# The recurrence's keys loaded once, operand splits spread among other work, and folded weights copied and stored in another way

## The chip, the core and the metric

The kernel runs on one core of a Trainium2 chip. The metric is the device time of one execution in microseconds (us). TensorE (PE in the profile) multiplies, VectorE (DVE), ScalarE (ACT) and GpSimd (POOL) work on tiles, and SP's queue issues most DMAs; ScalarE and GpSimd have DMA queues of their own, which issue a few. Each engine runs its instructions in the order in which they stand in its queue, and an instruction that waits holds what stands behind it.

## The reference, cut to what matters

One layer: a joint input projection, whose columns feed a sliding-window attention with sinks and a gated linear recurrence, an output projection, a cross-attention to 256 memory tokens, and a SwiGLU feed-forward. `T = 2048` tokens, `D = 1024`, float32.

```python
u = rms_norm(h, g_mix_pre);  z = u @ w_in
qa, ka, va, qh, fh, ih, gh = jnp.split(z, IN_SPLITS, axis=-1)
y = concat(swa_with_sinks(qa, ka, va, sinks), hgrn2(qh, fh, ih, gh, ...)) @ w_out
h = h + rms_norm(y, g_mix_post)
u = rms_norm(h, g_x_pre);  m = rms_norm(mem, g_mem)
h = h + rms_norm(cross_attention(u, m, wq_x, wk_x, wv_x, wo_x), g_x_post)
u = rms_norm(h, g_ffn_pre)
h = h + rms_norm((silu(u @ w_gate) * (u @ w_up)) @ w_down, g_ffn_post)
```

In the recurrence, per head and chunk of 64 tokens, with `b` the running sum of the log decays in the chunk:

```python
A = jnp.where(causal, einsum((qc * exp(b - b_mid)), (kc * exp(b_mid - b))), 0.0)
kv = einsum(kc * exp(b_last - b), vc)          # S = decay * S + kv
o = A @ vc + (qc * exp(b)) @ S_prev
```

## The kernel before, in words

Tokens are worked on in pairs of chunks, 128 tokens, `n = 0..15` (8 per half, "block" of 1024 tokens). Every float32 product is made of three products of float32r operands: an operand is split into an upper part, a rounded copy (`hi`), and a lower part, the difference (`lo`). The copy is an ACTIVATE on ScalarE or an operation on GpSimd, the difference is always on VectorE. A product of upper by upper, upper by lower and lower by upper goes into one PSUM bank (`mm3`, lines 170 to 172 for projections; `products`, lines 1107 to 1109 in the later stages).

The program has these stages, by time: the input projection of block 0 (`in_first`); the input projection of block 1 (`in_proj`) with the sliding-window attention (`swa`) and the recurrence (`hgrn`) of block 0 between its columns; the attention of block 1 beside the rest of `in_proj`; the recurrence of block 1 beside `fold_cross`; and then `phases`, a long run of products with the output projection, the folded cross-attention and the feed-forward, in a form with seven products where eight would be usual.

`fold_cross` multiplies weights by the normalised memory so that the cross-attention needs only two products per token: it normalises and transposes the memory into `mT` (lines 131 to 134), projects it with `wk_x` in 8 columns of 24 products of 256 columns each (line 150 splits the weight on ScalarE, line 153 on VectorE, lines 303 and 304 split the result `kv`), multiplies by `wq_x` into `qk_d` (line 326 copies the result into an `x` tile, line 328 stores it from ScalarE's queue), projects with `wv_x`, and multiplies by `wo_x` into `vo_d`: per head two rows of two banks, which line 364 copies into an `x` tile on ScalarE and line 365 stores from ScalarE's queue. Differences of parts of `qk` are stored in `qk_s` too.

`hgrn` takes one pair through several steps. In `hgrn_front`, `k1` and `kk` are two copies of the same keys, loaded from `z_d`; `k1` (one buffer) goes into the products with the queries (line 867), whose banks `copy_predicated` (line 868, VectorE) and a copy (line 869, ScalarE) empty into `atz`; `kk` is scaled in place on GpSimd (line 876) and transposed (line 879) into `kt` (line 881), the values `v` are transposed (line 884) into `vt` (line 886). `hgrn_state` multiplies `kt` by `vt` (line 896), `hgrn_out` and `hgrn_last` make the output.

`swa_back` copies its result into the tile `ys` (lines 833 and 834), which is stored to `y_d`; `ys` has one buffer. `w_sums` (line 1018) makes sums and differences of parts of `w_out`, in `x` tiles, and stores them in `w_s`.

`phases` begins with a prologue: eight steps that load halves of four operands of the output projection (`w_out` and `w_s`) into `z` tiles and split them into resident tiles `T` (lines 971 and 974). `mix` calls them after the recurrence. Then come the streamed operands, loaded from `y_d` into `sraw` tiles and split into `S`, which the first products of the stage need.

A scheduler sets the order of each queue: it takes instructions as their operands come ready in its own timeline and by the order in which they were traced, so that an instruction that is traced late can stand early. `mark()` notes the last instruction traced so far on ScalarE, VectorE, TensorE and SP, and what is traced inside `behind()` stays behind that instruction on each of these. A tile with `bufs=n` has n buffers, and a new tile waits until what used its buffer n tiles earlier is done. A PSUM bank is freed by the instruction that empties it. `io_tile("x")` has three buffers, `io_tile("z")` two.

Of the kernel before, what the change touches and what calls it, by code (L numbers as in the profile page):

```python
# [11 lines left out]
F32 = mybir.dt.float32  # L12
F32R = mybir.dt.float32r
I32 = mybir.dt.int32
AF = mybir.ActivationFunctionType
ALU = mybir.AluOpType
AX = mybir.AxisListType

P = 128
T = 2048  # L20
D = 1024
# [8 lines left out]
NT = T // P  # L30
# [3 lines left out]
C_KA, C_VA, C_QH, C_FH, C_IH, C_GH = 512, 640, 768, 1280, 1792, 2304  # L34
# [14 lines left out]
class Layer:  # L49
# [155 lines left out]
    def mix(self):  # L205
        tc, I = self.tc, self.I
        kw = dict(reuse_waits="tile")
        with contextlib.ExitStack() as left:
            def pool(name, at, **k):
                return at.enter_context(tc.tile_pool(name=name, bufs=1, **k, **kw))  # L210

            self.mc = pool("mc", left)
            self.r_x = self.cst.tile([P, NT], F32, name="r_x")
            with (
                tc.tile_pool(name="t1", bufs=3, **kw) as self.ts,
                tc.tile_pool(name="t2", bufs=3, **kw) as self.tb,
                tc.tile_pool(name="s1", bufs=2, side="right", **kw) as self.st_pool,
                contextlib.ExitStack() as at,
            ):
                self.banks(at, "ps1", **MOST)  # L220
                self.raws, self.parts, self.sums = 3, 3, 3
                u = self.in_first()
            self.banks(left, "ps2", **FOUR)
            self.hg = pool("hg", left)
            self.wp = pool("wp", left)
            self.io = pool("io", left)
            with tc.tile_pool(name="sw", bufs=1, side="right", **kw) as self.sw:
                self.zero_tiles()
                swa = self.swa(range(NPB), "st")
                hgrn = self.hgrn(range(NPB), "h")  # L230
                cols = self.in_proj(1, u)
                for _ in range(2):
                    next(cols)
                for _ in swa:
                    for _ in range(5):
                        next(hgrn)
                    next(cols)
                for _ in hgrn:
                    pass
                jobs = self.jobs()  # L240
                sums = self.w_sums()
                swa = self.swa(range(NPB, NT), "sth")
                for i, _ in enumerate(swa):
                    next(cols)
                    if i:
                        self.mark()
                        for _ in range(4):
                            next(sums, None)
                for _ in cols:
                    pass  # L250
                for _ in sums:
                    pass
            phases = self.phases(jobs, None, lambda: self.io_tile("z"))
            with tc.tile_pool(name="xp", bufs=1, side="right", **kw) as self.xp:
                fold = self.fold_cross()
                for i, _ in enumerate(self.hgrn(range(NPB, NT), "gt")):
                    for _ in range(1 if i % 5 else 0):
                        next(fold)
                for _ in range(8):
                    next(phases)  # L260
                for _ in fold:
                    pass
            left.close()
            with (
                tc.tile_pool(name="t3", bufs=3, **kw) as self.ts,
                tc.tile_pool(name="t4", bufs=3, **kw) as self.tb,
                tc.tile_pool(name="s3", bufs=2, side="right", **kw) as self.st_pool,
                contextlib.ExitStack() as at,
            ):
                self.banks(at, "ps3", **MOST)  # L270
                self.raws, self.parts, self.sums = 6, 4, 5
                for _ in phases:
                    pass
# [9 lines left out]
    def fold_cross(self):  # L283

        nc, ph = self.nc, self.xp
# [30 lines left out]
        for d in (0, 4, 1, 5, 2, 6, 3, 7):  # L316
            th, tl = self.wcols(self.I["wq_x"], d, "A")
            o = self.io_tile("x")
            for q in range(2):
                ps = self.bank("sh"[q])  # L320
                for r in range(2):
                    h = 2 * q + r
                    self.mm3(ps[:, r * M:(r + 1) * M],
                             [((th[:, j, :], tl[:, j, :]), (kT[0][:, j, :], kT[1][:, j, :])) for j in (2 * h, 2 * h + 1)])
                sl = slice(q * 512, (q + 1) * 512)
                nc.scalar.activation(o[:, sl], ps, AF.Copy, scale=gx[:, d:d + 1])
                if q:
                    self.put(self.qk_d[d * P:(d + 1) * P, :], o)
                yield
            if d < 4:  # L330
                upper = o
                continue
            a, b = [ph.tile([P, D], F32, tag="qs", name=f"qs{d}_{i}", bufs=2) for i in range(2)]
            l, r = slice(0, 512), slice(512, D)
            nc.vector.tensor_tensor(a[:, l], upper[:, r], upper[:, l], ALU.subtract)
            nc.vector.tensor_tensor(a[:, r], o[:, r], upper[:, r], ALU.subtract)
            nc.vector.tensor_tensor(b[:, l], a[:, r], upper[:, l], ALU.add)
            nc.vector.tensor_tensor(b[:, r], o[:, l], b[:, l], ALU.subtract)
            for c, t in enumerate((a[:, l], a[:, r], b[:, l], b[:, r])):
                self.store(self.qk_s[c, :, (d - 4) * 512:(d - 3) * 512], t)  # L340
        for vT in projected(self.I["wv_x"]):
            yield
        for h in range(4):
            banks = [[self.bank(k) for k in "sh"] for _ in range(2)]
            for i in range(2):
                j = 2 * h + i
                raw = raw_tile()
                self.load(raw, self.I["wo_x"][j * P:(j + 1) * P, :])
                wh, wl = split_tiles()
                self.split(raw, wh, wl, "A")  # L350
                for mt in range(2):
                    ms = slice(mt * P, (mt + 1) * P)
                    ah, al = vT[0][:, j, ms], vT[1][:, j, ms]
                    for q in range(2):
                        sl = slice(q * 512, (q + 1) * 512)
                        nc.tensor.matmul(banks[mt][q], ah, wh[:, sl], start=(i == 0), stop=False)
                        nc.tensor.matmul(banks[mt][q], ah, wl[:, sl], start=False, stop=False)
                        nc.tensor.matmul(banks[mt][q], al, wh[:, sl], start=False, stop=(i == 1))
                if i == 0:
                    yield  # L360
            for mt in range(2):
                o = self.io_tile("x")
                for q in range(2):
                    nc.scalar.activation(o[:, q * 512:(q + 1) * 512], banks[mt][q], AF.Copy)
                self.put(self.vo_d[(2 * h + mt) * P:(2 * h + mt + 1) * P, :], o)
            yield


# [440 lines left out]
    def swa_back(self, n, kinds, S, vs):  # L809
        nc, ph = self.nc, self.sw  # L810
        nk = len(vs)
        o = M - nk * P
        kinds = itertools.cycle(kinds)
        ys = ph.tile([P, 4, P], F32, tag="ys", name=f"ys{n}")
        for g in range(2):
            t = []
            for kb in range(nk):
                ps = self.bank(next(kinds))
# [18 lines left out]
    def hgrn_front(self, n, kinds, f):  # L837
# [5 lines left out]
        def get(t, c):  # L843
            self.load(t, z[c:c + 512, t0:t0 + P].rearrange("(h p) t -> p h t", p=P))
            return t

        def new(tag, bufs=1, w=P):
            return ph.tile([P, 4, w], F32, tag=tag, name=f"{tag}{n}", bufs=bufs)
# [1 line left out]
        def c8(ap):  # L850
            return ap.rearrange("p h (c t) -> p (h c) t", t=64)

        k1 = get(new("k1"), C_FH)
        qq = new("qq", 2, 192)
        q1 = get(qq[:, :, 0:P], C_QH)
        kk = get(new("kk"), C_FH)
        v = get(new("v"), C_IH)
        g1 = self.G1[:, n, :].unsqueeze(2).broadcast_to([P, 4, 64])

# [13 lines left out]
        nc.gpsimd.tensor_tensor(q6.rearrange("p h (c t) -> p h c t", t=64), q1.rearrange("p h (c t) -> p h c t", t=64),  # L873
                                self.G[:, n, :, :].unsqueeze(3).broadcast_to([P, 4, 2, 64]), ALU.mult)

        nc.gpsimd.tensor_tensor(kk[:, :, 0:64], kk[:, :, 0:64], g1, ALU.mult)
        ps = self.bank(next(kinds))
        for h in range(4):
            nc.tensor.transpose(ps[:, h * P:(h + 1) * P], kk[:, h, :], self.ident)
        kt = new("kt")  # L880
        nc.scalar.activation(kt, ps.rearrange("p (h t) -> p h t", h=4), AF.Copy)
        ps = self.bank(next(kinds))
# [305 lines left out]
    def phases(self, jobs, first, prologue=None):  # L1188
# [50 lines left out]
        def split(g):  # L1239

            if pending and pending[0][0] <= g:
                _, k, f = pending.pop(0)
                f()
                left[k] -= 1
                return True
            return False
# [58 lines left out]

        if not first:
            for i in range(8):
                half(-1, prologue)
                split(len(steps))
                yield  # L1310
        stream(0)
        yield
# [458 lines left out]
```

## Time and profile before

| | us |
|---|---|
| median of 3 runs (2566.24 to 2569.68) | 2568.44 |
| the profiled execution's own time | 2568.33 |
| its span, from the first to the last instruction | 2566.6 |
| VectorE busy in the span | 1754.7 (68%) |
| ScalarE busy | 1254.0 (49%) |
| GpSimd busy | 457.5 (18%) |
| DMA packets' share of 16 engines on SP's queue, 443.76 MB | 51.6% |
| on ScalarE's queue, 8.39 MB | 0.8% |

The windows of the profile show one stretch of time each, with the busy time of each engine in it and the mean clock that TensorE was granted (1.00 is full speed). A row of waits names the waiting engine and line, and the engine and line that ended the wait. In a row of a group of instructions the time behind the second bar is how long the engine stood idle just ahead of them and what ended it. A tile's name stands without its buffer number.

### The profile page before, as it was taken

To read this page: it belongs to the slowest core of one execution; us is meant where nothing else is said; L and a number is where in the kernel's file an instruction comes from. 1 tells how busy PE (TensorE), PEld (TensorE's weight loads), DVE (VectorE), ACT (ScalarE), POOL (GpSimd) and SP (SyncE) were. 2 spreads that over 40 slices of the span, in tenths; PEclk is the share of its full clock that TensorE was granted. 3 is DMA by queue.
4 is the path that set the end of the run, shared out by engine and by line. 5 is a ranking of instruction groups with operands and counts; after the bars stand their busy time and mean duration, and the time that the engine had idled before them with its cause. 6 is when DMAs were issued, how large, how long until landed. Compare 5 with 4: busy or idle time off the path is not lost.

```text
span 2566.6 us, 34125 instructions
## 1 busy us (share of the span) xinstructions
PE 2516.8 (98%) x12012; PEld 2097.4 (82%) x12012; DVE 1754.7 (68%) x2805; ACT 1254.0 (49%) x2614; POOL 457.5 (18%) x633
## 2 busy tenths in 40 slices
PE   8999999998999999999999999999999999999998
PEld 7777888887997888888788888888888888888886
DVE  6868588788667578787775665585566566664756
ACT  5454365656555566565564333353333344543543
POOL 2233333322312343224210000000000000000022
PEclk9999999999999999999999999999999999999999
DMA  6254555466896796768983542253555433566798
GB/s 238 100 204 138 175 161 170 151 200 205 269 322 216 225 279 207 262 227 209 303 267 115 177 160 74 84 196 135 179 203 181 164 128 137 201 211 191 224 224 205
DMA packets 277834, 495.22 MB, mean 193 GB/s; under 512 B 20896, under 2 KB 135584, under 8 KB 277152
## 3 DMA queue, kind: packets, MB, share of 16 engines
q1 hardware_dynamic: 264128, 443.76, 51.6%
q0 software_dynamic: 11232, 40.90, 8.4%
q10 hardware_dynamic: 2304, 8.39, 0.8%
q8 instruction: 94, 1.54, 0.2%
q14 instruction: 76, 0.62, 0.1%
HBM read 330.45 MB, written 162.53 MB: 192 GB/s over the span
## 4 chain that ended last, share of the span: by engine, by line
PE 82%; DMA 6%; issue 5%; DVE 4%; ACT 2%; POOL 1%; SPq 0%; POOLq 0%; DVEq 0%; ACTq 0%
PE psm L1107 21%; PE psm L1109 21%; PE psm L1108 21%; PE psg L172 3%; PE psg L170 3%; PE psg L171 3%; PE pss L1360 1%; DMA row<-in_x_dram 1%; DMA row<-h_d 1%; DMA row<-y_d 1%; DVE S L974 1%; DMA y_d<-row 1%; ACT junk L1449 1%; PE pss L820 0%; PE pst L820 0%
## 5 line engine op out<-in xcount | busy, mean ns | idle before, releaser
L1107 PE MATMUL psm<-T,S 128*128 128x512 f32 x2744 | 1063.8, 392 | 13.4 <-ACT part L1122 5.1
L1108 PE MATMUL psm<-T,S 128*128 128x512 f32 x2744 | 1071.4, 391 | 0.0
L1109 PE MATMUL psm<-T,S 128*128 128x512 f32 x2744 | 1064.9, 391 | 3.3 <-DVE S L974 3.2
L1107 PEld LDWEIGHTS psm<-T,S 128*128 128x128 f32 x2744 | 516.6, 188 | 125.9 <-ACT part L1122 7.9
L1109 PEld LDWEIGHTS psm<-T,S 128*128 128x128 f32 x2744 | 516.3, 188 | 113.5 <-DVE S L974 5.9
L1108 PEld LDWEIGHTS psm<-T,S 128*128 128x128 f32 x2744 | 516.5, 188 | 106.5
L971 ACT ACTIVATE S<-sum 128x512 fp32r<-128x512 f32 (+1 forms) x336 | 206.2, 618 | 326.9 <-PE psm L1109 323.7
L974 DVE TENSOR_TENSOR S<-sraw,S 128x512 fp32r<-128x512 f32 (+1 forms) x312 | 211.2, 684 | 214.3 <-ACT S L971 199.8
L974 DVE TENSOR_TENSOR S<-sum,S 128x512 fp32r<-128x512 f32 (+1 forms) x400 | 272.8, 686 | 82.0 <-ACT S L971 65.0
L1122 ACT ACTIVATE part<-psm 128x512 f32<-128x512 f32 x294 | 173.1, 592 | 183.2 <-PE psm L1109 178.8
L971 ACT ACTIVATE S<-sraw 128x512 fp32r<-128x512 f32 (+1 forms) x271 | 165.8, 617 | 159.4 <-PE psm L1109 142.8
L1478 POOL DMA_DIRECT2D row<-y_d x28 | 25.0, 893 | 1071.4 <-DMA sraw<-hid_d 905.3
L1449 ACT ACTIVATE junk<-row 128x512 f32<-128x512 f32 x160 | 99.7, 625 | 104.4 <-DVE row L1471 35.2
L170 PE MATMUL psg<-u,whi 128*128 128x512 f32 x352 | 143.7, 408 | 3.9 <-DVE z L693 2.1
L974 DVE TENSOR_TENSOR T<-row,T 128x1024 fp32r<-128x1024 f32 x104 | 123.4, 1194 | 30.8 <-ACT T L971 30.5
L172 PE MATMUL psg<-u,wlo 128*128 128x512 f32 x352 | 142.0, 403 | 0.5 <-DVE wlo L153 0.5
L171 PE MATMUL psg<-u,whi 128*128 128x512 f32 x352 | 141.2, 401 | 0.0
L971 ACT ACTIVATE T<-row 128x1024 fp32r<-128x1024 f32 x104 | 105.4, 1023 | 23.1 <-DMA row<-in_w_down_dram 10.3
L1653 DVE TENSOR_TENSOR part<-psm,part 128x512 f32<-128x512 f32 x66 | 45.5, 689 | 65.5 <-PE psm L1109 65.4
L973 POOL TENSOR_SCALAR S<-sum 128x512 fp32r<-128x512 f32 x64 | 50.8, 795 | 217.7 <-PE psm L1109 151.6
L153 DVE TENSOR_TENSOR wlo<-raw,whi 128x1024 fp32r<-128x1024 f32 x54 | 68.7, 1273 | 28.3 <-ACT whi L150 20.1
L1644 DVE TENSOR_TENSOR row<-psm,part 128x512 f32<-128x512 f32 x66 | 45.5, 689 | 57.2 <-PE psm L1109 57.1
(337 smaller groups left out, 3471.7 us busy)
## 6 DMA issues: line engine op xcount, KB each, us to landing
sraw<-in_w_gate_dram SPq DMA_DIRECT2D x44, 512.0 KB, 4.9
sraw<-in_w_up_dram SPq DMA_DIRECT2D x44, 512.0 KB, 4.9
hid_d<-row SPq DMA_DIRECT2D x44, 512.0 KB, 2.7
h_d<-row SPq DMA_DIRECT2D x32, 512.0 KB, 6.8
y_d<-row SPq DMA_DIRECT2D x32, 512.0 KB, 3.9
sraw<-hid_d SPq DMA_DIRECT2D x32, 512.0 KB, 5.9
row<-h_d POOLq DMA_DIRECT2D x30, 512.0 KB, 8.0
row<-y_d POOLq DMA_DIRECT2D x28, 512.0 KB, 7.6
```

What stands on the lines that cost most here:

```text
L153: nc.vector.tensor_tensor(lo, raw, f32(hi), ALU.subtract)
L170: nc.tensor.matmul(ps, ah, bh, start=(i == 0), stop=False)
L171: nc.tensor.matmul(ps, ah, bl, start=False, stop=False)
L172: nc.tensor.matmul(ps, al, bh, start=False, stop=(i == n - 1))
L971: self.nc.scalar.activation(hi, raw, AF.Copy)
L973: self.nc.gpsimd.tensor_scalar(hi, raw, 1.0, 1.0, ALU.mult, ALU.mult)
L974: self.nc.vector.tensor_tensor(lo, raw, f32(hi), ALU.subtract)
L1107: nc.tensor.matmul(ps, s[:, 0, k, :], t[:, 0, k, :], start=st, stop=False, **kw)
L1108: nc.tensor.matmul(ps, s[:, 0, k, :], t[:, 1, k, :], start=False, stop=False, **kw)
L1109: nc.tensor.matmul(ps, s[:, 1, k, :], t[:, 0, k, :], start=False, stop=sp, **kw)
L1122: nc.scalar.activation(t, ps, AF.Copy)
L1449: self.nc.scalar.activation(junk, a, AF.Square, scale=float(D) ** -0.5, accum_out=to)
```

## The change

Five edits, in `mix`, `fold_cross`, `swa_back`, `hgrn_front` and `phases`:

1. The first step of `fold_cross` is traced ahead of the recurrence of block 1, and the eight prologue steps of `phases` are traced one by one at every fourth step of that recurrence, each behind what has been traced by then (`mark`, `behind`).
2. Of the upper four row blocks of `qk_d`, only the left half is stored (a quarter of it is left out; the later stages read differences from `qk_s` in its place).
3. The second row of each head's `vo` goes into a `z` tile, the second half of every row is copied by VectorE, and the rows are stored from SP's queue.
4. The last pair's `ys` is part of an `x` tile.
5. `kk` is gone: `k1` gets two buffers, is scaled in place after its products, and is then transposed.

```diff
@@ mix
                 fold = self.fold_cross()
+                next(fold)
                 for i, _ in enumerate(self.hgrn(range(NPB, NT), "gt")):
                     for _ in range(1 if i % 5 else 0):
                         next(fold)
-                for _ in range(8):
-                    next(phases)
+                    if i % 4 == 2 and 2 < i < 36:
+                        self.mark()
+                        next(phases)
                 for _ in fold:
                     pass
@@ fold_cross
                 if q:
-                    self.put(self.qk_d[d * P:(d + 1) * P, :], o)
+                    cols = slice(0, 512 if d < 4 else D)
+                    self.put(self.qk_d[d * P:(d + 1) * P, cols], o[:, cols])
                 yield
...
             for mt in range(2):
-                o = self.io_tile("x")
-                for q in range(2):
-                    nc.scalar.activation(o[:, q * 512:(q + 1) * 512], banks[mt][q], AF.Copy)
-                self.put(self.vo_d[(2 * h + mt) * P:(2 * h + mt + 1) * P, :], o)
+                o = self.io_tile("xz"[mt])
+                nc.scalar.activation(o[:, 0:512], banks[mt][0], AF.Copy)
+                nc.vector.tensor_copy(o[:, 512:D], banks[mt][1])
+                self.store(self.vo_d[(2 * h + mt) * P:(2 * h + mt + 1) * P, :], o)
             yield
@@ swa_back
-        ys = ph.tile([P, 4, P], F32, tag="ys", name=f"ys{n}")
+        ys = (ph.tile([P, 4, P], F32, tag="ys", name=f"ys{n}") if n < NT - 1 else
+              self.io_tile("x")[:, 0:512].rearrange("p (h t) -> p h t", h=4))
@@ hgrn_front
-        k1 = get(new("k1"), C_FH)
+        k1 = get(new("k1", 2), C_FH)
         qq = new("qq", 2, 192)
         q1 = get(qq[:, :, 0:P], C_QH)
-        kk = get(new("kk"), C_FH)
         v = get(new("v"), C_IH)
...
-        nc.gpsimd.tensor_tensor(kk[:, :, 0:64], kk[:, :, 0:64], g1, ALU.mult)
+        nc.gpsimd.tensor_tensor(k1[:, :, 0:64], k1[:, :, 0:64], g1, ALU.mult)
         ps = self.bank(next(kinds))
         for h in range(4):
-            nc.tensor.transpose(ps[:, h * P:(h + 1) * P], kk[:, h, :], self.ident)
+            nc.tensor.transpose(ps[:, h * P:(h + 1) * P], k1[:, h, :], self.ident)
@@ phases
         if not first:
             for i in range(8):
-                half(-1, prologue)
-                split(len(steps))
+                with self.behind():
+                    half(-1, prologue)
+                    split(len(steps))
                 yield
```

The scheduler moves instructions on every engine between the start of the recurrence and the first steps of `phases`. Three places follow. Line numbers of the changed kernel are 1 to 4 higher than those of before. The first is ScalarE's queue at the end of the attention and the start of the fold, before the change (`T<-z` is an operand split of the prologue, `pth` and `ys` belong to the attention, `whi` to the fold, `z<-psg` to the input projection, `atz`, `kt` and `vt` to the recurrence):

```order
L824 ACTIVATE pth_11_6138<-pst_6133 128x512
L971 ACTIVATE T_7770<-z_7771 128x1024
L833 ACTIVATE ys_6098<-psh_6117 64x512
L824 ACTIVATE pth_00_6225<-pss_6220 128x512
L824 ACTIVATE pth_01_6234<-pst_6229 128x512
L833 ACTIVATE ys_6098<-psh_6142 64x512
L824 ACTIVATE pth_10_6250<-pss_6245 128x512
L971 ACTIVATE T_7770<-z_7776 128x1024
L150 ACTIVATE whi_6591<-raw_6589 128x1024
L688 ACTIVATE z_6343<-psg_6371 128x512
L824 ACTIVATE pth_11_6259<-pst_6254 128x512
L869 ACTIVATE atz_2019<-psg_6412 64x2x64
```

And ScalarE's queue from the same bank's release on, after the change:

```order
L872 ACTIVATE atz_2019<-psg_6470 64x2x64
L837 ACTIVATE x_6203<-psh_6222 64x512
L884 ACTIVATE kt_6502<-psg_6497 128x512
L872 ACTIVATE atz_2019<-pst_6475 64x2x64
L837 ACTIVATE x_6203<-psh_6247 64x512
L133 ACTIVATE mT_6392<-pss_6404 128x4x128
L133 ACTIVATE mT_6392<-pss_6428 128x4x128
L889 ACTIVATE vt_6509<-pst_6504 128x512
```

No split of the prologue stands ahead of that release any more; the first two come after the second and the third column of the fold, and `mT` comes ahead of `vt`. The second place is VectorE's queue at the same point, after the change (`x<-x,x` is the last sum of `w_sums`, `mT` there is its lower part, `x<-psh,x` is the last pair's `ys`):

```order
L871 COPY_PREDICATED atz_2019<-cmask,pst_6475 128x256
L838 TENSOR_TENSOR x_6203<-psh_6222,x_6203 64x512
L1021 TENSOR_TENSOR x_6317<-x_6317,x_5981 128x1024
L838 TENSOR_TENSOR x_6203<-psh_6247,x_6203 64x512
L871 COPY_PREDICATED atz_2021<-cmask,pst_6583 128x256
L134 TENSOR_TENSOR mT_6393<-pss_6404,mT_6392 128x4x128
L134 TENSOR_TENSOR mT_6393<-pss_6428,mT_6392 128x4x128
L134 TENSOR_TENSOR mT_6393<-psh_6411,mT_6392 128x4x128
```

Before, that sum stood some twenty instructions earlier in VectorE's queue, ahead of the attention's last normalisation, and four splits of the prologue stood between the rows shown. The third place is SP's queue at the end of the fold, before the change (`raw` is a weight of the fold, `sraw` the first operand of the next stage; the stores to `vo_d` are in ScalarE's queue):

```order
L75 DMA raw_8058<-in_wo_x_dram 128x1024
L75 DMA raw_8088<-in_wo_x_dram 128x1024
L75 DMA raw_8106<-in_wo_x_dram 128x1024
L75 DMA sraw_8150<-y_d 128x2x512
L75 DMA sraw_8152<-y_d 128x2x512
L75 DMA sraw_8154<-y_d 128x2x512
```

And after the change:

```order
L75 DMA raw_8056<-in_wo_x_dram 128x1024
L75 DMA raw_8074<-in_wo_x_dram 128x1024
L78 DMA vo_d<-x_7996 128x1024
L78 DMA vo_d<-z_8000 128x1024
L78 DMA vo_d<-x_8044 128x1024
L78 DMA vo_d<-z_8048 128x1024
L78 DMA vo_d<-x_8092 128x1024
L75 DMA sraw_8118<-y_d 128x2x512
L78 DMA vo_d<-z_8096 128x1024
L75 DMA sraw_8120<-y_d 128x2x512
L75 DMA sraw_8122<-y_d 128x2x512
```

The first `sraw` load now stands behind seven of the eight stores to `vo_d`, two of which (rows 7948 and 7952) stand ahead of the weights shown, and the second load behind the eighth.

## The prediction

> **What bounds the kernel now.** I read the page's first lines, then the windows of 20 us around the stage that the change touches, then what TensorE waited for there.
>
> ```profile
> PE 2516.8 (98%) x12012; PEld 2097.4 (82%) x12012; DVE 1754.7 (68%) x2805; ACT 1254.0 (49%) x2614; POOL 457.5 (18%) x633
> ```
>
> TensorE is busy for all but 50 of 2566.6 us, so only its idle time and its clock can be won. The changed kernel's instructions stand in the old order up to about 285 us and from about 800 us on, on all engines; the windows between are what counts. Columns: TensorE busy, its weight loads, VectorE, ScalarE, GpSimd, granted clock, share of the DMA engines, GB/s.
>
> ```profile
> 600.00:620.00 20.00, 17.93 (x92) 14.59 (x91) 19.27 (x42) 10.81 (x30) 5.80 (x7) 1.00 1.04 337
> 620.00:640.00 20.00, 15.59 (x83) 13.01 (x82) 13.68 (x27) 10.04 (x18) 1.10 (x4) 0.87 0.46 133
> 640.00:660.00 20.00, 17.25 (x116) 16.00 (x115) 11.64 (x19) 11.76 (x27) 8.04 (x10) 0.88 1.00 304
> 660.00:680.00 20.00, 20.00 (x173) 20.00 (x173) 14.10 (x19) 12.08 (x27) 4.82 (x5) 1.00 0.72 229
> 720.00:740.00 20.00, 19.88 (x170) 19.56 (x169) 15.10 (x21) 12.24 (x34) 6.29 (x8) 1.00 1.05 388
> 760.00:780.00 20.00, 18.34 (x78) 14.16 (x77) 6.13 (x5) 10.56 (x16) 0.00 (x0) 1.00 0.90 307
> 780.00:800.00 20.00, 18.11 (x79) 14.34 (x78) 16.30 (x24) 10.06 (x19) 3.37 (x4) 1.00 0.92 330
> ```
>
> Two places lose time: 620 to 660, where the attention ends and the fold begins (idle 4.41 + 2.75 = 7.2 us, and clock (0.13 + 0.12) x 20 = 5.0 us, together 12.2), and 760 to 800, the fold's tail and the passage to the next stage (1.66 + 1.89). Between them TensorE is full. The waits behind this, in the order total, times, longest:
>
> ```profile
> PE psg L879 <- ACT atz L869: 4.4, 1, 4.4
> PE pst L884 <- DMA v<-z_d: 2.2, 1, 2.2
> PE psm L1107 <- ACT S L971: 1.9, 1, 1.9
> PE pss L356 <- ACT x L364: 1.7, 2, 1.0
> PE pss L171 <- DVE mT L134: 0.5, 1, 0.5
> ```
>
> ScalarE caused the 4.4 us: it stood in its queue behind an operand split of the prologue.
>
> ```profile
> L971 ACT ACTIVATE T<-z 128x1024 fp32r<-128x1024 f32 x8 | 8.5, 1057 | 10.2 <-DMA z<-in_w_out_dram 8.3 <-DMA z<-w_s 1.9
> 633.93 1.06 ACT L971 ACTIVATE T<-z 128x1024 fp32r<-128x1024 f32 x1 [3.07 <-DMA z<-in_w_out_dram]
> 636.79 0.26 ACT L869 ACTIVATE atz<-psg 64x128 f32<-64x128 f32 x1
> ```
>
> All eight splits lie between 600 and 670, and ScalarE stood 10.2 us for their loads; the copy that frees TensorE's bank came only after one of them.
>
> **The change, part by part.** The sum is made against the profiled execution's own 2568.33 us (span 2566.6), which is 0.11 below the median of 2568.44.
>
> *Splits spread, and the fold's first step ahead of the recurrence: -8.3.* The order shows no split left ahead of the copy at L869, and the first two come after two fold columns. So the 4.4 us go. The 2.2 us for `v` go too: ahead of the transposes of pair 9 the new order has 72 fold products of 256 columns.
>
> ```profile
> 641.24 6.02 DMA v<-z_d
> 655.46 0.28 PE L171 MATMUL pss<-mT,whi 128*128 128x256 f32 x1
> 655.58 0.28 PE L172 MATMUL pss<-mT,wlo 128*128 128x256 f32 x1
> ```
>
> At 0.12 us from one to the next they are some 8.5 us, against a load of 6. What is late next follows from the new order's queues. These rows of groups, from the windows between 600 and 680, price them (busy, mean ns):
>
> ```profile
> L833 ACT ACTIVATE ys<-psh 64x512 f32<-64x512 f32 x6 | 3.6, 592 | 0.1
> L133 ACT ACTIVATE mT<-pss 128x512 fp32r<-128x512 f32 x2 | 1.2, 588 | 0.0
> L1018 DVE TENSOR_TENSOR x<-x,x 128x1024 f32<-128x1024 f32 x2 | 3.3, 1644 | 0.0
> L834 DVE TENSOR_TENSOR ys<-psh,ys 64x512 f32<-64x512 f32 x6 | 4.1, 684 | 0.3 <-ACT ys L833 0.3
> L134 DVE TENSOR_TENSOR mT<-pss,mT 128x512 fp32r<-128x512 f32 x2 | 1.4, 684 | 0.0
> x<-in_w_out_dram SPq DMA_DIRECT2D x1, 512.0 KB, 6.1
> ```
>
> First, pair 8's state product waits for `vt`, which on ScalarE stands behind one bank release, one L833 and two L133 (about 0.3 + 0.6 + 1.2) and takes 0.6; TensorE has some 1.5 us of other work meanwhile, which leaves about 1.2. Second, the fold's first products need the lower parts of `mT`. On VectorE they now stand behind the last sum of L1018 (whose operand is loaded behind the store of the attention's pair 14, 6.1 us), one L834 and one bank release: 1.6 + 0.7 + 0.4 + two L134 of 0.7 = 4.1, against 1.8 of TensorE work, 2.3 left. Third, the last L134 comes two VectorE operations later, about 0.4 beyond the first half of products. That is 3.9 us of new waits; 12.2 - 3.9 = 8.3. Bounds: 12.2 if all are covered, 4.4 if only the wait for ScalarE goes. I count no lost clock for these three: the wait of 1.9 us at 781 left the clock at 1.00 in its window.
>
> The same eight splits now lie between 640 and 740, where TensorE hardly waits. They add 8 x 1.06 us to ScalarE, which is busy 12 of each 20 us there: 60% becomes 70%. Cover is there, but each split can wait for its load again, with the fold's own splits queued behind:
>
> ```profile
> L150 ACT ACTIVATE whi<-raw 128x1024 fp32r<-128x1024 f32 x8 | 8.4, 1052 | 2.3 <-PE pss L171 1.3 <-PE psh L171 0.7 <-PE psg L171 0.2
> ```
>
> I take *+1.0*, between 0 and the 10.2 that all eight cost ScalarE before.
>
> *Keys loaded once, a quarter of `qk_d` not stored, the last `ys` in another tile: 0.*
>
> ```profile
> L876 POOL TENSOR_TENSOR kk<-kk,G 128x256 f32<-128x256 f32 x8 | 6.2, 772 | 26.1 <-DMA kk<-z_d 26.1
> kk<-z_d SPq DMA_DIRECT2D x16, 256.0 KB, 4.3
> qk_d<-x ACTq DMA_DIRECT2D x8, 512.0 KB, 6.3
> ```
>
> 5.2 of 495 MB go, but TensorE waited for none of them; 26.1 us of waiting for `kk` are GpSimd's. In exchange the scaling (0.77 us) can't start before the four products that read the unscaled keys. At pair 8, the tightest, TensorE has three products of 512 columns (0.23 us each, by the rows at 780 us below) and four transposes between; elsewhere at least twenty products. Covered but for a few tenths at pair 8; uncovered it would be 0.77 a pair, 12 in all. Behind it on GpSimd stand attention sums and in_proj's splits, for which VectorE and TensorE wait; GpSimd is busy 5.8 of 20 us in that stage's last window, so they have room. The `ys` tile's store was waited for by ScalarE alone and is in the first term.
>
> *Half of the `vo_d` copies on VectorE, five tiles: -1.7.* In the tail ScalarE copied four banks per head, and stood for a tile:
>
> ```profile
> 775.63 0.60 ACT L364 ACTIVATE x<-pss 128x512 f32<-128x512 f32 x1 [3.44 <-DMA vo_d<-x]
> ```
>
> VectorE is idle over half of 760 to 780 (6.13 busy of 20), so the two waits of L356 (1.7) go. Bounds 0 and 1.7.
>
> *The `vo_d` stores moved to SP's queue: +7.6.* This is the dear part. SP issues in order. Before, the first `y_d` load of the next stage was issued 13 us before the fold's last matmul:
>
> ```profile
> 767.80 0.38 SPq L75 DMA_DIRECT2D sraw<-y_d  x1
> 780.31 0.39 PE L357 MATMUL psh<-wlo,kv 128*128 128x512 f32 x1
> 780.54 0.40 PE L358 MATMUL psh<-whi,kv 128*128 128x512 f32 x1
> 781.71 0.33 ACTq L84 DMA_DIRECT2D vo_d<-x  x1
> 782.83 0.50 PE L1107 MATMUL psm<-T,S 128*128 128x512 f32 x1 [1.89 <-ACT S L971]
> DMA to landing us min/median/max: 3.6/5.8/10.5
> sraw<-in_w_gate_dram SPq DMA_DIRECT2D x44, 512.0 KB, 4.9
> ```
>
> In the new order that load stands behind seven of the eight stores, and the seventh waits for the copies of the last head's first half, whose products end 0.9 us before the fold does. The copy (0.6) brings it to the fold's end; the load is issued 0.45 us after that. Loads of this tile here took 3.6 to 10.5 us; with one store ahead of it I take the 4.9 of the same size in the page. Then the split, 0.62, and two hand-overs, about 0.1 together: 6.1 us of idle TensorE in place of 1.9, so +4.2. An idle time that long also costs clock:
>
> ```profile
> PE psm L1107 <- ACT part L1122: 3.8, 1, 3.8
> 140.00:150.00 10.00, 6.22 (x24) 4.71 (x23) 8.73 (x12) 6.68 (x12) 3.95 (x8) 0.83 0.15 56
> 150.00:160.00 10.00, 10.00 (x37) 7.98 (x37) 5.09 (x8) 3.19 (x6) 1.63 (x3) 0.83 0.67 213
> ```
>
> After 3.8 us of idling, 0.17 x 20 = 3.4 us of clock were lost. +4.2 + 3.4 = +7.6; from +2.9 (landing in 3.6, no clock lost) to +13.2 (10.5). By the Trainium skill ("TensorE: Matmul & The Clock Gate", Part 1: The HAM clock gate) the clock is halved in windows of about 3.4 us, so that one cold window costs 1.7 us; an estimate by that page makes the sum 2565.2. The row here shows twice that, and the row decides.
>
> **Sum:** 2568.33 - 8.3 + 1.0 + 0 - 1.7 + 7.6 = 2566.9 us, within 0.2% of the time before, about what a measurement of this kernel can tell from no change.
>
> **Rivals.**
>
> *The stores hold nothing up* (the load lands in time, or the idle time is too short for the clock): without the 7.6 the sum is 2559.3, faster by 0.36%. For it: the wait there is 1.9 us now, and copies and loads have been moving ahead of the fold's end. Against it: the order itself, which puts the load behind a store whose data exist only at the fold's end. The Trainium skill ("DMA: Bandwidth & Descriptors", Issuing engines are not separate DMA queues) says that DMAs from SP, ScalarE and GpSimd run on the same 16 engines and interleave whichever engine started them. By that rule the move costs 8 x 0.33 us of SP's time and this rival is right; no run here shows the move yet, and the rule says nothing of an issuer that waits.
>
> *The spread splits stall the fold* (the slower side). Place: the eight splits among the fold's columns. Price: if each stands for its load as before, 10.2 us of ScalarE, and a column of 24 products takes 2.8 us, of which ScalarE needs 1.05 for L150 beside two or three copies of 0.3 to 0.6, so the cover is about 1 us a split. It decides when loads land more than that after their split's turn; then up to 10.2 us reach TensorE in place of my 1.0, and the time is 2576.1, slower by 0.3%. For it: DMA shares of 0.72 to 1.05 in these windows. Against it: loads are issued two splits ahead, some 12 us, and 2 MB of `kk` go from the same 100 us.
>
> *The change does not do what it says*: the scheduler puts the splits together again, or trades one wait for another, and 2568.3 stays. Against it: the order has them apart.
>
> **How the numbers follow.** Forecast 0.45; stores harmless 0.33; splits stall 0.16; nothing changes 0.06. Forecast and the last are within 0.2% (0.51), the first rival is faster (0.33), the second slower (0.16). The forecast's own range is 2563 (start term 12.2) to 2572.5 (landing in 10.5 us). Taking in the rivals and the bounds of their terms, with no more than 2 in 10 left out: 2557 to 2577.
>
> **What would show it.** Start term: the transposes of the keys no longer wait for L869's successor, the clock is 1.00 from 632 to 660, and waits of 1 to 2 us stand behind `vt` and `mT`. Store term: the first product of the next stage idle for about 6 us behind the load of `sraw`, and a clock under 0.9 in the 20 us after; a wait under 2.5 us there proves it wrong and the first rival right. Splits: TensorE's idle time between 650 and 740 stays under 2 us; over 5 speaks for the second rival. DMA total 490 MB, queue of ScalarE 3.1 MB. A new wait before 600 us would make the whole sum wrong, since I cost that stage at nothing.

## The result, and the profile after

The changed kernel takes 2561.55 us (median of 9 runs, 2559.27 to 2565.53) against 2568.68 us for the kernel before beside it (2565.82 to 2572.59). The ratio is 0.9975, with a 95% interval from 0.9966 to 0.9984: faster by 6.4 us, between 4.1 and 8.7. The forecast was 2566.9, 1.4 us less than before. The profiled run of the changed kernel took 2559.88 us.

The page's first lines and two of its rows on DMA queues (packets, MB, share):

```profile
PE 2510.6 (98%) x12012; PEld 2095.5 (82%) x12012; DVE 1758.5 (69%) x2813; ACT 1248.5 (49%) x2606; POOL 457.1 (18%) x633
...
DMA packets 269386, 489.97 MB, mean 192 GB/s; under 512 B 20640, under 2 KB 127136, under 8 KB 268704
...
q10 hardware_dynamic: 1152, 3.15, 0.3%
```

The traffic is what the change says: 490 MB in place of 495, and 3.15 MB left on ScalarE's queue. The windows of the changed kernel, with the columns of those shown of before:

```profile
620.00:640.00 20.00, 19.07 (x121) 16.40 (x120) 16.29 (x33) 11.90 (x24) 3.75 (x5) 1.00 0.50 142
640.00:660.00 20.00, 18.89 (x163) 18.68 (x162) 11.12 (x16) 9.02 (x20) 4.57 (x6) 1.00 0.91 255
660.00:680.00 20.00, 19.23 (x161) 18.83 (x160) 12.33 (x19) 12.10 (x34) 9.62 (x12) 1.00 0.80 251
700.00:720.00 20.00, 18.78 (x157) 18.43 (x156) 16.77 (x24) 14.53 (x36) 9.54 (x10) 1.00 1.04 368
760.00:780.00 20.00, 13.32 (x51) 10.36 (x50) 6.79 (x10) 6.15 (x9) 0.00 (x0) 0.85 0.74 266
780.00:800.00 20.00, 20.00 (x88) 16.51 (x87) 19.22 (x27) 11.79 (x20) 3.03 (x4) 0.98 0.79 285
```

Between 620 and 660 the clock is 1.00 now, where it was 0.87 and 0.88, and TensorE is busy for 38.0 of 40 us in place of 32.8. The price stands at the end of the fold: 6.7 us idle between 760 and 780, and a clock of 0.85. The waits of TensorE between 605 and 800 us in the changed kernel:

```profile
PE psg L899 <- ACT vt L889: 2.0, 2, 1.1
PE psg L882 <- POOL k L879: 1.2, 1, 1.2
PE psg L929 <- ACT atz L872: 0.8, 1, 0.8
PE psm L1110 <- ACT S L974: 6.7, 1, 6.7
```

Before, the same stretch had 4.4 (ScalarE's copy behind a split), 2.2 (`v`), 1.7 (the tail's copies), 1.9 (`S`) and about a microsecond of small ones. Rows of TensorE's timeline show how far the work had come in each kernel, first before and then after the change:

```profile
605.23 0.50 PE L170 MATMUL psg<-u,whi 128*128 128x512 f32 x1 [2.07 <-DVE z L693]
780.54 0.40 PE L358 MATMUL psh<-whi,kv 128*128 128x512 f32 x1
```

```profile
604.42 0.50 PE L170 MATMUL psg<-u,whi 128*128 128x512 f32 x1 [2.07 <-DVE z L696]
769.32 0.39 PE L361 MATMUL psh<-whi,kv 128*128 128x512 f32 x1
776.39 0.80 PE L1110 MATMUL psm<-T,S 128*128 128x512 f32 x1 [6.68 <-ACT S L974]
```

At 605 us the changed kernel was 0.8 us ahead. TensorE's order differs from 309 us on, but a lead of 0.7 is there at 231 us already (a wait that ends at 230.32 in place of 231.05), so that much is chance. At the fold's last product it was 11.2 us ahead (780.54 against 769.32): the fold's stage gained 10.4. At the first product of the next stage it was 6.4 ahead (782.83 against 776.39).

### The profile page after: what moved, and what is told of

The parts are those of the page before. It is cut to its first block, busy times and chain, and to the rows that moved or that the text cites. A ratio compares the mean times of both kernels' runs of the same rounds, so it can differ in the third digit from the quotient of the medians.

```text
span 2558.2 us, 34111 instructions
## 1 busy us (share of the span) xinstructions
PE 2510.6 (98%) x12012; PEld 2095.5 (82%) x12012; DVE 1758.5 (69%) x2813; ACT 1248.5 (49%) x2606; POOL 457.1 (18%) x633
## 3 DMA queue, kind: packets, MB, share of 16 engines
q10 hardware_dynamic: 1152, 3.15, 0.3%
```

## The experiments

The twelve were timed in three sets of four, each set on another chip and beside the kernel before on that chip. Ratios are to that kernel, with 95% intervals; microseconds worked out from a ratio go by its median, 2568.2 to 2569.1. Medians of different sets compare less well than ratios.

**The stores' place.** Three kernels change where the folded weights `vo_d` are stored from. In the first, GpSimd issues them:

```diff
-                self.store(self.vo_d[(2 * h + mt) * P:(2 * h + mt + 1) * P, :], o)
+                self.store_late(self.vo_d[(2 * h + mt) * P:(2 * h + mt + 1) * P, :], o)
```

> The changed kernel with the eight vo_d stores issued from GpSimd's queue, which is empty there, in place of SP's. If SP's order makes the wait of 6.7 us (my store term): the sraw loads are issued before the fold ends, the first product of the next stage waits about 1 us (ScalarE has one copy and one split behind the last product), no slow products follow (2.2 us in the changed kernel), and the time is 2561.5 - 5.7 - 2.2 = about 2554. If the stores hold nothing up and the load is late for another reason (rival): the wait stays at 6 to 7 us and the time at 2561.

Measured: 2556.96 us, ratio 0.9954 (0.9942 to 0.9967). SP's loads, TensorE's start of the stage, and its wait there:

```profile
755.00 4.96 SPq L75 DMA_DIRECT2D sraw<-y_d  x6
769.86 0.50 PE L1110 MATMUL psm<-T,S 128*128 128x512 f32 x1 [0.79 <-ACT S L974]
```

The six loads are issued from 755.0 on, 13.7 us before the fold's last product, and the wait falls from 6.7 to 0.8. In the changed kernel the first of them went out behind the seventh store:

```profile
769.57 0.32 SPq L78 DMA_DIRECT2D vo_d<-x  x1
769.99 0.39 SPq L75 DMA_DIRECT2D sraw<-y_d  x1
775.71 0.63 ACT L974 ACTIVATE S<-sraw 128x512 fp32r<-128x512 f32 x1 [5.78 <-DMA sraw<-y_d]
```

So SP's order made the wait, as forecast: the seventh store issued at 769.57, the load 0.42 us behind it, the split 5.7 us later. By its ratio this kernel is 0.0021 below the changed kernel, 5.4 us; the trace had 7.8 to give (5.9 of wait and 1.9 of slow products), which the intervals allow, and I had expected 2554.

In the second only the last head's two stores left SP, for ScalarE's queue:

```diff
+                (self.put if h == 3 else self.store)(self.vo_d[(2 * h + mt) * P:(2 * h + mt + 1) * P, :], o)
```

> The changed kernel with only the last head's two vo_d stores back on ScalarE's queue; the other six stay on SP's. If what counts is that the load stands behind a store whose data exist only at the fold's end: the loads go out after the third head's stores, the wait falls to about 1.9 us (two issues of 0.33 us stand ahead of the split on ScalarE), the slow products go, and the time is about 2554.5. If all six other stores delay SP as well (rival): the wait stays above 4 us and the time above 2558.

Measured: 2558.37 us, ratio 0.9964 (0.9950 to 0.9977). The wait at the stage's start:

```profile
PE psm L1110 <- ACT S L974: 2.6, 1, 2.6
```

With the six other stores still on SP the loads go out behind them from 764.78 on, in place of 755.0, and 1.8 us more of the wait is left than with none there. The other 4.1 of the 5.9 us, and the slow products, go with the last head's stores, whose data exist only at the fold's end. The time is 4 us above the 2554.5 that I expected. The third is the kernel before with edit 3 alone:

> The kernel before with edit 3 alone (five tiles, half of the copies on VectorE, stores on SP's queue). My terms: -1.7 for the tail's copies, +4.8 for the wait (6.7 in place of 1.9) and about +2 for slow products: 2568.5 + 5.1 = about 2573.5, with the wait of 6 to 7 us at the start of the next stage. If the stores are harmless without the earlier fold (rival): 2567, wait under 2.5 us.

Measured: 2571.12 us, ratio 1.0011 (1.0003 to 1.0020), slower by 2.8 us where I expected 5.1. Its wait there:

```profile
PE psm L1107 <- ACT S L971: 6.8, 1, 6.8
```

The wait is as forecast, so edit 3 alone is a loss, by less than I had summed.

**The fold's start.** First the kernel before with edit 1 alone (the early first step, and the spread prologue):

```diff
                 fold = self.fold_cross()
+                next(fold)
...
-                for _ in range(8):
-                    next(phases)
+                    if i % 4 == 2 and 2 < i < 36:
+                        self.mark()
+                        next(phases)
```

> The kernel before with edit 1 alone (first step of the fold ahead of the recurrence, prologue steps spread). If the splits in ScalarE's queue cost the 4.4 us and the clock after it: the wait of the keys' transposes for L869 is gone, the clock is 1.00 from 620 to 660, and the time is 2568.5 - 8 to 10 = about 2559. If the gain comes from the keys that are loaded once, through 4 MB less traffic (rival): the loads of v are still late, and the time is 2566 or more.

Measured: 2566.14 us, ratio 0.9997 (0.9988 to 1.0007): nothing. Its waits and one window:

```profile
PE pst L886 <- DMA v<-z_d: 5.0, 1, 5.0
PE psg L928 <- ACT atz L871: 1.9, 1, 1.9
PE psg L898 <- ACT vt L888: 1.7, 1, 1.7
PE pss L359 <- DVE wlo L153: 1.7, 1, 1.7
```

```profile
640.00:660.00 20.00, 16.82 (x130) 0.83 0.88 193
```

(Columns of the window, here TensorE alone: busy, clock, DMA share, GB/s.) The 4.4 us behind `atz` are gone, as I had reasoned, but the load of `v` is late by 5.0 us and the clock is down. In this kernel's order the transposes of `v` stand ahead of the fold's 72 products; in the changed kernel these products stand ahead and cover the load. Which edit moves them? The order changes with edit 4 alone, the last pair's `ys` in an `x` tile, so that went in beside edit 1:

```diff
-        ys = ph.tile([P, 4, P], F32, tag="ys", name=f"ys{n}")
+        ys = (ph.tile([P, 4, P], F32, tag="ys", name=f"ys{n}") if n < NT - 1 else
+              self.io_tile("x")[:, 0:512].rearrange("p (h t) -> p h t", h=4))
```

> The kernel before with edits 1 and 4 (first fold step early, prologue spread, last ys in an x tile). With edit 1 alone the transposes of v of pair 9 stood ahead of the 72 fold products and waited 5.0 us for their load; with edit 4 the order has the 72 products ahead of them. Theory: edit 4 moves these products, so the wait of 5.0 us and the slow products after it go, the clock is 1.00 from 620 to 660, and the time is about 2560. Rival (the double load of the keys is what makes v late): the wait for v stays at 2 us or more, and the time at 2564 to 2566.

Measured: 2563.36 us, ratio 0.9974 (0.9964 to 0.9984), 3 us above what I expected. Its window and waits:

```profile
640.00:660.00 20.00, 18.63 (x159) 1.00 1.04 282
```

```profile
PE psg L899 <- ACT vt L889: 3.5, 3, 1.7
PE pss L359 <- DVE wlo L153: 1.8, 2, 1.2
PE psg L929 <- ACT atz L872: 1.3, 1, 1.3
```

No wait for `v` is left, the clock is full, and the interval lies clear of that of edit 1 alone. Edit 1 needs edit 4 here; edit 4 alone was not run. The changed kernel without edit 4 is the check from the other side:

> The changed kernel with edit 4 undone (the last pair's ys is a tile of its own again). The order has the transposes of v ahead of the fold's products again. Theory: a wait for v of 2 to 5 us and 1 to 2 us of slow products come back, about 2565.5. Rival (keys loaded once are enough): no wait for v over 0.5 us, and the time stays at 2561.5.

Measured: 2563.36 us, ratio 0.9980 (0.9970 to 0.9990). The wait for `v` is back:

```profile
PE pst L886 <- DMA v<-z_d: 2.2, 1, 2.2
```

The mechanism holds, and the fold's stage takes 2.5 us longer in the trace than in the changed kernel, but the loss in time, 0.0005, is within the intervals. And the changed kernel without edit 1, that is with the old lines of `mix` and without `behind`:

> The changed kernel with edit 1 undone: the prologue's eight splits stand together again between 620 and 670, the first of them ahead of ScalarE's copy at the bank's release. My prediction: the wait of 4.4 us and its slow products come back, 2561.5 + 6 to 8 = about 2568.5. Rival (edit 4 alone gains what is gained there, since the fold's products now stand ahead of what waits): the wait is under 2 us and the time about 2562.

Measured: 2567.02 us, ratio 0.9999 (0.9988 to 1.0009). The wait that the spreading removes is back, with the split ahead of it on ScalarE:

```profile
PE psg L880 <- ACT atz L870: 4.0, 1, 4.0
```

```profile
634.56 1.06 ACT L972 ACTIVATE T<-z 128x1024 fp32r<-128x1024 f32 x1 [3.22 <-DMA z<-in_w_out_dram]
```

Without edit 1, with edit 4 still in, all that the change gains in time is lost: from the product at 605 us to its last one the fold's stage takes 174.5 us here, 175.3 before and 164.9 in the changed kernel.

**The keys and the quarter.** The changed kernel with `kk` loaded and scaled beside `k1` again:

```diff
-        k1 = get(new("k1", 2), C_FH)
+        k1 = get(new("k1"), C_FH)
...
+        kk = get(new("kk"), C_FH)
...
-        nc.gpsimd.tensor_tensor(k1[:, :, 0:64], k1[:, :, 0:64], g1, ALU.mult)
+        nc.gpsimd.tensor_tensor(kk[:, :, 0:64], kk[:, :, 0:64], g1, ALU.mult)
```

> The changed kernel with edit 5 undone (kk is loaded and scaled beside k1 again, 4 MB more). My prediction counts this edit at nothing: 2561.5, with the 72 products still ahead of the transposes of v. Rival (the traffic counts): loads of v or kk come late between 640 and 740, TensorE waits 2 us or more for them there, and the time is 2564 or more.

Measured: 2566.52 us, ratio 0.9991 (0.9982 to 1.0000). My zero was wrong here. Two waits of TensorE in the stage, and what VectorE stood for:

```profile
PE psh L359 <- DVE kv L306: 3.1, 1, 3.1
PE pst L871 <- issue: 2.3, 1, 2.3
```

```profile
DVE sg L931 <- DMA sg<-z_d: 7.6, 2, 3.9
```

The recurrence's last pairs come later in this kernel (their two loads of `sg` are issued at 741.4 and 749.2; in the changed kernel at 736.2 and 743.1). VectorE stands 7.6 us for them (4.2 in the changed kernel), with the fold's splits and `kv` queued behind, and TensorE runs out of operands. The time and TensorE's waits are of the size that the rival named, but come through VectorE's queue, and it is not shown that traffic is the cause. The 2.3 us behind "issue" end with the load of the keys for that pair:

```profile
697.82 0.37 SPq L75 DMA_DIRECT2D k<-z_d  x1
702.65 0.56 PE L871 MATMUL pst<-qq,k 128*128 128x192 f32 x2 [2.29 <-issue]
```

It landed 4.7 us after its issue, just ahead of the product. In the changed kernel the load for the same products was issued at 685.56, 15 us ahead of them and ahead of the previous pair's products at 689.55, which its second buffer allows. Undoing edit 5 takes that buffer away together with the single load, and no run separates the two. The other way round, edits 1, 4 and 5 put into the kernel before:

> The kernel before with edits 1, 4 and 5; beside e5 only the keys' single load is added. My prediction counts that at nothing: 2563.4 as in e5. What the changed kernel without edit 5 showed (loads of sg for the gate that come late behind kk's loads, VectorE behind, TensorE waiting 5.3 us for both between 700 and 757): the waits of 1.7, 1.3 and 1.2 us that e5 has at 700, 711 and 755 go, and the time is about 2558.5.

Measured: 2560.63 us, ratio 0.9971 (0.9962 to 0.9981), between the two expectations and not to be told from the kernel with edits 1 and 4. Of the waits that I expected to go, those near 700 and 711 went (0.3 at 706 is left); that for `wlo` at 755 stayed, and a tail wait came:

```profile
PE pss L358 <- ACT x L366: 2.5, 1, 2.5
PE pss L359 <- DVE wlo L153: 1.8, 1, 1.8
```

ScalarE stood 5.3 us for a tile there, which is what edit 3's five tiles remove. So edit 5 seems to be worth something beside edit 3; its size beside the other edits alone stays open. Edit 2 was undone in the kernel with the GpSimd stores:

```diff
-                    cols = slice(0, 512 if d < 4 else D)
-                    self.put(self.qk_d[d * P:(d + 1) * P, cols], o[:, cols])
+                    self.put(self.qk_d[d * P:(d + 1) * P, :], o)
```

> The kernel of the GpSimd stores with edit 2 undone (all of qk_d stored, 1 MB more). My prediction counts the quarter at nothing: 2557, with no new wait of TensorE over 1 us between 680 and 760. Rival (ScalarE or the DMA engines are short there): waits of 2 us or more behind ScalarE's copies into x, 2559 or more.

Measured: 2555.53 us, ratio 0.9948 (0.9935 to 0.9960), no slower than with the quarter left out (0.9942 to 0.9967). It had one wait of 1.4 us at 759.6 behind a copy into `x`, where I expected none over 1. This and the first kernel above are the fastest that I found, and they can't be told apart.

**What happens to a late start.** In the changed kernel's trace, 4 us were gained between the first 20 products of the next stage and the end, where the order of the work is the same as before. One explanation is that loads and splits get ahead while TensorE stands. To try it, six copies that serve nothing went into ScalarE's queue of the GpSimd kernel, ahead of the stage's first splits:

```diff
+                if h == 3 and mt:
+                    idle = self.io_tile("z")
+                    for _ in range(6):
+                        nc.scalar.activation(idle, o, AF.Copy)
+                    self.mark()
...
-            upto(i)
+            with contextlib.nullcontext() if first else self.behind():
+                upto(i)
```

> The kernel of the GpSimd stores with six copies of 128x1024 put on ScalarE ahead of the first splits of the next stage (6.4 us of work that is of no use): the stage starts about 7 us late and on a slow clock, as in the changed kernel, without any store on SP. If a late start is partly made good behind it, since loads and splits get ahead meanwhile: the start is 8 us later than without the copies, and the end only 4 to 5, so about 2561.5. If nothing is made good (rival): 2557 + 8 = 2565.

Measured: 2566.25 us, ratio 0.9991 (0.9983 to 1.0000). The wait became longer than meant:

```profile
PE psm L1115 <- ACT S L979: 10.8, 1, 10.8
```

The start's price in the trace is 10.8 - 0.8 of wait and 1.9 of slow products, 11.9 us; in time it is 9.3 by medians, 9.5 by ratios, and the two intervals together leave 5.6 to 13.3. My theory, that some half is made good, is not borne out: about four fifths arrive at the end, though the noise would still allow a half. Last, the changed kernel once more:

> The changed kernel again, on the chip of these runs. 2561.5; the wait of 6.7 us at the next stage's start and ten to eleven slow products behind it as in the first profile. From the stage's 20th product to 1300 us the changed kernel's first profile gained 2.9 us on the kernel before: if a late start is made good there, this profile shows 2 to 3 us again; if that was chance, anything from -1 to +1.

Measured: 2562.03 us, ratio 0.9974 (0.9963 to 0.9985), and the stage's start again:

```profile
PE psm L1110 <- ACT S L974: 6.7, 1, 6.7
```

From 800 to 1300 us this profile gained 4.4 us on that of before, where the first one gained 2.9. So the gain shows twice in this kernel. But other kernels with a late start scatter, from gains of about 2.6 (the six copies, edit 3 alone) to a loss of 1.0 (without edit 4). From one wait that all profiles share, at 1175 to 1195 us, to the end, equal work took 1375 to 1382 us in the fourteen profiles: differences of a few microseconds there are the chance of one execution. I take no part of the result from that stretch. In three comparisons the time shows less of the start's price than the trace, 5.4 of 7.8 us (stores from GpSimd), 2.8 of 5.9 (the last head's from ScalarE) and 9.5 of 11.9 (the six copies), none of them clear of the noise; whether a part of a late start is made good stays open.

## Why the prediction was right or wrong

**What bounds the kernel** held: the fold's stage and its two ends decide. No new wait came before 600 us.

**Start of the fold, splits and tail: -9.0 forecast together, -10.4 measured** (11.2 less the 0.8 of 605 us), and about -11.2 in the second profile. Of the 10.4, 5.3 are waits (9.3 before, 4.0 after); the other 5.1 are what slow products cost before, which I had priced at 5.0. In the profile of edit 3 alone, whose fold starts as before, that remainder is 2.4, so it is not the same in every execution. The size is right. Two of the parts are not, and their errors went opposite ways, so that the sum came this near is partly luck. The wait behind `vt` was 0.86 (forecast 1.2). The 2.7 us for the lower parts of `mT` did not come: the chain on VectorE took about as long as forecast, until 637.6, but TensorE itself reached those products only at 638.3. The spread splits may have cost up to three times my 1.0. This row of the changed kernel, between 640 and 740 us, shows ScalarE standing 11.0 us for their loads, as against 10.2 before:

```profile
L974 ACT ACTIVATE T<-z 128x1024 fp32r<-128x1024 f32 x8 | 8.5, 1064 | 12.6 <-DMA z<-in_w_out_dram 11.0 <-DMA k<-z_d 1.6
```

Of its 12.6 us at most 3.1 reached TensorE, as waits of 1.1, 0.8 and 1.2 at 655, 663 and 707; that is over the 2 us that I had set as a sign. Two splits stood about 4 us for their loads (4.2 and 3.9), which met the second rival's condition, but its price of up to 10.2 was not paid: there was more cover than the 1 us a split that I had reckoned. The tail's 1.7 went, as forecast.

**The reason given for the start was incomplete.** I put the 2.2 us for `v` down to edit 1, whose early first step I took to bring the 72 products forward. Edit 1 alone left them behind the transposes and made that wait 5.0 us, and its time did not move. The smallest edit, one tile for the last `ys`, moves the products. I had read the new order for what stands where, and not asked which edit put it there.

**Keys at nothing: wrong, as far as the runs tell.** I looked for the cost in TensorE's and GpSimd's waits for `kk`, and counted the load and the scaling but not the second buffer of `k1`. Undone in the changed kernel, the edit shows elsewhere: a load of keys comes late, and the recurrence falls behind the fold. That cost 4 us by ratios, 0.9991 against 0.9975 (or 0.9974), with intervals that overlap by 0.0002 or 0.0003. Whether the buffer or the single load is what counts was not tried. **The quarter at nothing:** nothing was measured.

**Stores on SP: the mechanism was right, and the price of its clock was mis-sized.** Forecast: 6.1 us of wait and 3.4 of clock, in all +7.6. Measured: 6.68 of wait in place of 1.89, +4.8, and slow products that cost 1.9 more than before. The wait is longer than forecast because the load's split began 5.7 us after the issue, where I had taken 4.9 for the landing. These rows, of the changed kernel, show the step from one product to the next before and after the clock came back:

```profile
776.98 0.63 PE L1111 MATMUL psm<-T,S 128*128 128x512 f32 x1
777.41 0.63 PE L1112 MATMUL psm<-T,S 128*128 128x512 f32 x1
...
781.36 0.39 PE L1110 MATMUL psm<-T,S 128*128 128x512 f32 x1
781.59 0.40 PE L1111 MATMUL psm<-T,S 128*128 128x512 f32 x1
```

A step is 0.43 us in place of 0.23. The first eleven steps cost 2.2 us too much, against 0.4 before: 4.8 + 1.9 = 6.7. The 3.4 came from windows: 0.15 x 20 + 0.02 x 20 is 3.4 here too, but part of the slow time is idle time, in which a slow clock costs nothing. In time, moving these stores off SP was worth 5.4 us by ratios, 4.6 by medians. The Trainium skill ("TensorE: Matmul & The Clock Gate", Part 1: The HAM clock gate) gives half clock in windows of about 3.4 us, an estimated 1.7 us for one; the slow products cost 1.8 to 2.7 us in the seven profiles with a wait over 6 us, so that page came nearer than my windows.

**The rivals.** "The stores hold nothing up" gave 2559.3, and the time, 2561.55, lies nearer to that than to the forecast, and below the forecast's own range (2563 to 2572.5); but its reason is wrong, since the wait of 6.7 us is there. The rule behind it ("DMA: Bandwidth & Descriptors" of the Trainium skill, Issuing engines are not separate DMA queues) speaks of transfers that share 16 engines. What decided here was the queue of the engine that issues: the same transfers issued from GpSimd took the wait away.

**The sum.** The forecast's terms come to -1.4. The measured ones, -10.4 + 6.7 = -3.7 (and -4.2 in the second profile), stand against a time that fell by 4.1 to 8.7. So the places of the gain and the loss were right, and the sum was too small a gain: by 1.4 us in the fold's stage, by 0.9 in the store term. Two to three us more have no place that I can show; the 2.9 and 4.4 us that the two profiles gained between 800 and 1300 us may hold them. That the wide range, 2557 to 2577, takes in the result is partly luck: its lower end stands there for the first rival, whose reason did not hold.

## What to carry to other kernels

A store that is moved to an in-order queue costs what stands behind it there: look up which of the next stage's loads wait behind the last store, and give such stores a queue with nothing else in it, as GpSimd's was here (0.9954 in place of 0.9975). When several edits move one schedule, read the order of each edit alone before booking a gain to one of them; here the smallest edit moved the products that covered a load. Price a slow clock by the step between products where that can be read: the window with idle time in it gave 3.4 us for 2.2 at the next stage's start, though 5.0 for 5.1 at the fold's.

## What was not expected of the hardware

What a wait costs in clock behind it does not simply grow with the wait. In all seven profiles with a wait of 6.5 to 10.8 us at the stage's start, the first product of 128x512 was followed after 0.59 us, and the next seven to eleven ran at steps of 0.43 in place of 0.23, 1.8 to 2.7 us too much in all, and the longest wait cost no more than the others (2.25). In five profiles with waits of 0.8 to 2.6 us only the first three steps were long (0.34, 0.39, 0.34), 0.4 us too much in all. But in two, the kernels before with edit 1 and with edits 1 and 4, a wait of 2.3 and 2.2 us cost as much as a long one, 2.0 and 1.7 us; in the first of them the slow steps began only six products after the wait. This is the start in the kernel with edits 1 and 4, then in the one whose last head's stores left SP:

```profile
775.82 0.68 PE L1110 MATMUL psm<-T,S 128*128 128x512 f32 x1 [2.24 <-ACT S L974]
776.29 0.63 PE L1111 MATMUL psm<-T,S 128*128 128x512 f32 x1
776.72 0.63 PE L1112 MATMUL psm<-T,S 128*128 128x512 f32 x1
```

```profile
771.65 0.50 PE L1110 MATMUL psm<-T,S 128*128 128x512 f32 x1 [2.59 <-ACT S L974]
771.99 0.40 PE L1111 MATMUL psm<-T,S 128*128 128x512 f32 x1
772.38 0.50 PE L1112 MATMUL psm<-T,S 128*128 128x512 f32 x1
```

A step of 0.47 and 0.43 us follows a wait of 2.24, and one of 0.34 and 0.39 a wait of 2.59. What tells the two cases apart was not tried.
